# A list scheduler that models TensorE's tiles and keeps a sum of activity, and a state scaled on ScalarE

## The chip, the core and the metric

The kernel runs on one core of one Trainium2 chip. The metric is the device time of one execution in microseconds. Before the change three runs took 1821.65, 1817.13 and 1821.46 us, a median of 1821.46.

## What is computed

One layer of a hybrid trunk is applied to 512 tokens of a sample (with cached context) and to 128 tokens of a prompt, 640 rows of 1024 channels in all, in float32. In the reference, cut to what matters:

```
h   = rmsnorm(x) * (1 + scale1) + shift1                 # scale, shift, gate from silu(c) @ ada_w
u   = h @ w_in                                           # all branches' inputs and gates
y_a = latent attention(u)        y_b = mLSTM(u), both directions
y_c = windowed attention(u)      y_d = RWKV-7(u), both directions
x   = x + gate1 * ((sum of sigmoid(gate_i) * (y_i @ w_o_i)) @ w_out)
x   = x + gate2 * (relu(h2 @ mlp_w1)**2 @ mlp_w2)        # h2: the norm of the new x
```

The RWKV branch holds a 64 x 64 state S per head and direction, advanced token by token:

```
S_new = S * w_t - (S @ kh_t) (a_t kh_t)^T + v_t k_t^T,   y_t = S_new @ r_t
```

The last states and caches of the prompt are outputs too.

## The kernel before

Dense products are done three times with float32r operands: an operand is cut into a high part (`wh`, `yh`, `HH`) and the rest (`wl`, `yl`, `HL`), and high x high, high x low and low x high are summed (`mm3`). A weight tile comes by DMA into one of three buffers `wr`, ScalarE casts it to `wh` (line 589), and POOL for the first 139 tiles, VectorE for the others, forms `wl` (line 592); both have six buffers. `dense_b` (tiles `pb`, 320 columns), `dense_t` (`pt`, 208 to 264 columns) and `dense_a` (`pa`, 512 columns) then run the matmuls. Projections of `h` read `HH` and `HL`. Small products (RWKV, attention's probabilities, transposes) are plain float32 matmuls; the profile lists each of these as two instructions where it isn't a transpose.

The RWKV branch takes heads in pairs `hp`, each in two directions. `rwkv_prep` makes decayed keys, their products (`pat`, `pkb`, `pbs`) and masks; `rwkv_inverse` and `rwkv_comb` invert 32 x 32 blocks (`ptp`, `px`); `rwkv_chain` walks the chunks of 64 tokens. One `step` of it (from line 1100; 80 in all, 20 per pair, in four interleaved sequences) multiplies the old state `so_` (128 x 128, two heads) by `KR`, adds `Am` x `VU` on a 64 x 64 tile, copies the result to `W1` (ScalarE, line 1115), multiplies it on a 64 x 64 tile, negates it into `VU` (VectorE, line 1118), then runs four matmuls on 128 x 64 tiles, two for the output `ys` (ScalarE, line 1127) and two for the state. Line 1109 scales the old state by the decay `DL` into the new one `sn`, and line 1124 (VectorE) adds the product to it.

What sets the order of all this is a planner, `order`, at the end of the build. It reads every instruction, finds what each must wait for, gives it a duration (`cost`), and plays the program through: at each moment the engine that is free first takes, of its instructions whose inputs are there, the one with the longest path `bl` to the end. The resulting order per engine is written into the program; the chip runs each engine's queue in it. TensorE has one more rule: the planner adds up columns (`cols`) in the ticks of a fixed grid (`TICK`), holds TensorE to be slow in a tick when the one before had under 3060 (`warm`), and where the present tick seems to fall short it picks the matmul with the most columns per time. Conflicts of matmuls on the same rows and columns of the array are modelled in `busy`; a change of tile costs nothing, and the next matmul may be chosen 0.02 us after the last began. Projections that nothing needs soon (`late`, the gates above all) are put between the RWKV, mLSTM and attention work in this way.

Of the kernel before, what the change touches and what calls it, by code (L numbers as in the profile page):

```python
# [2 lines left out]

# [10 lines left out]
AF = mybir.ActivationFunctionType  # L14
ALU = mybir.AluOpType
# [19 lines left out]

LAT = {"PE": 0.3, "DVE": 0.195, "Activation": 0.195, "Pool": 0.195}
TO_PE = 0.127
DMA_START, DMA_END, DMA_RATE, DMA_GAP = 1.5, 0.95, 360e3, 0.641


# [86 lines left out]
def cost(i, eng, op, pools):  # L127

    ins = [q for q in i.ins if hasattr(q, "bass_ap")]
    outs = [q for q in i.outs if hasattr(q, "bass_ap")]  # L130

    def free(q):
        n = 1
        for s, c in list(q.ap)[1:]:
            n *= c
        return n

    def psum(q):
        t = pools.tiles.get(q.bass_ap.tensor.name)
        return t is not None and "PSUM" in t[0].space  # L140

    if op == "InstMatmult":
        n, m, k = free(outs[0]), list(outs[0].ap)[0][1], list(ins[0].ap)[0][1]
        if "is_transpose=True" in str(i):
            return 0.109
        if "float32r" in str(i.ins[0].dtype):
            return max(n / 2400, 0.107) + 0.003
        return max(n / 600, 0.05) + 0.002
        
    n = max([free(q) for q in ins + outs] or [1])  # L150
    if eng == "Activation":
        if op == "InstLoadActFuncSet":
            return 1.28
        return (0.051 if psum(ins[0]) else 0.094) + n / 1200 + 0.093 * (len(ins) + len(outs) - 2)
    if eng == "DVE":
        if op == "InstTensorScalarPtr":
            return 0.13 + n / 960 if 'is_scalar_tensor_tensor=True' in str(i) else 0.068 + n / (960 if psum(ins[0]) else 1920)
        if op == "InstTensorCopy" and not psum(ins[0]):
            return 0.068 + n / 1920
        return 0.066 + n / 960  # L160
    if eng == "Pool":
        if op == "InstDMACopy":
            return 1.04
        return 0.15 + n / (480 if op == "InstTensorTensor" else 240 if op == "InstTensorScalarPtr" else 800)
    return 0.05


def order(tc, pools):
    raw = list(tc.nc.cur_bb.bb.instructions)
    N = len(raw)  # L170
    eng = [str(i.engine).split(".")[-1] for i in raw]
    op = [type(i).__name__ for i in raw]
    live = [o != "BassTilePoolBoundary" for o in op]
    dur = [cost(i, e, o, pools) if l else 0.0 for i, e, o, l in zip(raw, eng, op, live)]
# [26 lines left out]
    for k, i in enumerate(raw):  # L201
# [11 lines left out]
        for q, wr in seq:  # L213
# [3 lines left out]
            t = pools.tiles.get(name)  # L217
# [10 lines left out]
            p0, p1, m = regions(q, dram)  # L228
            w, r = acc.setdefault(name, ([], []))
# [87 lines left out]
    while st:  # L317
        a = st.pop()
# [6 lines left out]
    for a in reversed(topo):  # L325
        x = 0.0
# [74 lines left out]
    for a in spot:  # L401
        q, i = raw[a].outs[0], raw[a].ins[0]
        n = 1
        for s, c in list(q.ap)[1:]:
            n *= c
        passes = 2 if "is_transpose=True" in str(raw[a]) else 1 if "float32r" in str(i.dtype) else 4
        cols[a] = passes * n * (spot[a][1] - spot[a][0]) / 128
    warm = lambda t: seen.get(int(t / TICK) - 1, 0) >= 3060
    while left:
        best = None  # L410
        for e in ENG:
            if avail[e]:
                t = free[e]
            elif future[e]:
                t = max(free[e], future[e][0][0])
            else:
                continue
            if best is None or t < best[0]:
                best = (t, e)
        t, e = best  # L420
        while future[e] and future[e][0][0] <= t + 1e-9:
            r, a = heapq.heappop(future[e])
            heapq.heappush(avail[e], (-bl[a], a))
        j = 0
        if e == "PE" and (0.937 or 0) and len(avail[e]) > 1:
            gap = 3060 - seen.get(int(t / TICK), 0)
            if (not warm(t) and 0) or gap > ((int(t / TICK) + 1) * TICK - t) * 2400 * 0.937 > 0:
                j = max(range(len(avail[e])), key=lambda i: (cols[avail[e][i][1]] / dur[avail[e][i][1]], -avail[e][i][0]))
        if j:
            _, a = avail[e].pop(j)  # L430
            heapq.heapify(avail[e])
        else:
            _, a = heapq.heappop(avail[e])
        start[a] = t
        if isdma[a]:
            by = 4
            for s, c in list(raw[a].outs[0].ap):
                by *= c
            if list(raw[a].outs[0].ap)[-1][1] < 128:
                by *= 2  # L440
            if e == "SP":
                hw = t + (DMA_GAP if raw[a].ins[0].bass_ap.tensor.name in pools.tiles and "DRAM" not in pools.tiles[raw[a].ins[0].bass_ap.tensor.name][0].space else 0.606)
            else:
                hw = t + 1.04
            b0 = max(bus, hw + DMA_START)
            bus = b0 + by / DMA_RATE
            fin = bus
            free[e] = hw
        else:
            if e == "PE":  # L450
                r0, r1, c0, c1 = spot[a]
                t = max([t] + [x[4] for x in busy if x[0] < r1 and r0 < x[1] and x[2] < c1 and c0 < x[3]])
                start[a] = t
                w = warm(t)
                fin = t + dur[a] * (1 if w else 2)
                k, x = int(t / TICK), t
                while x < fin:
                    y = min(fin, (k + 1) * TICK)
                    seen[k] = seen.get(k, 0) + cols[a] * (y - x) / (fin - t)
                    k, x = k + 1, y  # L460
                busy = [x for x in busy if x[4] > t + 0.02] + [(r0, r1, c0, c1, fin)]
                free[e] = t + 0.02
            else:
                fin = free[e] = t + dur[a]
        out[e].append(a)
        left -= 1
        for tl in of[a]:
            tdone[tl] = max(tdone.get(tl, 0.0), fin + (DMA_END if isdma[a] else 0.13))
            nuse[tl] -= 1
            if nuse[tl] == 0:  # L470
                P, key, _ = pools.tiles[tl]
                q = tags[id(P), key]
                heapq.heappush(q[0], (tdone[tl], tl))
                grant(q)
        for b, l in succ[a]:
            ready[b] = max(ready[b], (t if l < -1 else fin + l))
            need2[b] -= 1
            if need2[b] == 0:
                release(b)
    info = mybir.DependencyInfo(mybir.DependencyClass.NoSync, mybir.DependencyReason.DATA)  # L480
    for e in ENG:
        for a, b in zip(out[e], out[e][1:]):
# [41 lines left out]
def build(nc, tc, I, O):  # L524
# [562 lines left out]
    def rwkv_chain(units):  # L1087
# [13 lines left out]
        def step(ui, i):  # L1101
# [4 lines left out]
            sn = S[ui, sq] = stile()  # L1106
            VU = rp.tile([128, 128], F32, tag="VU", bufs=4, name=nm("VU"))
            SY.dma_start(VU[0:64, :], vscr[c * 64 : c * 64 + 64, ts_(hp)])
            G.tensor_scalar(sn, so_, DL[:, c : c + 1], None, op0=ALU.mult)  # L1109
            ps = mps.tile([128, 512], F32, tag="pc", bufs=PC, name=nm("pst"))  # L1110
            mm(ps[:, 0:128], KR[:, c, :], so_, start=True, stop=False)
            for h in range(2):
# [771 lines left out]
```

## Time and profile before

| | |
|---|---|
| median of three runs | 1821.46 us |
| profiled execution | 1829.33 us, span 1827.4 us |
| mean granted TensorE clock | 0.960 |
| TensorE busy | 1742.4 us, 95% |
| weight loads busy | 1551.1 us, 85% |
| VectorE busy | 968.7 us, 53% |
| ScalarE busy | 716.9 us, 39% |
| POOL busy | 471.9 us, 26% |

A busy time is the union of an engine's instructions; matmuls overlap, so a busy TensorE can still be a slow one, and starts a known distance apart tell more. The granted clock is a share of full speed. In groups of instructions `out<-in` are the program's tile names, then shapes and the count, busy time and the mean of one, and last the idle time of the engine before them with whom it waited for.

### The profile page before, as it was taken

What the parts mean: (1) busy time and instruction counts of PE and PEld (TensorE: products, weight loads), DVE (VectorE), ACT (ScalarE), POOL (GpSimd) and SP (SyncE); (2) the same over time, 40 slices, a digit from 0 to 9 for tenths busy, and PEclk for the clock granted to TensorE, in tenths of its full rate; (3) what the DMA queues carried; (4) which work ended last, traced back from release to release, by engine and by line L of the source; (5) the groups of instructions that cost most, each with busy time, mean ns of one, the idle gap of its engine ahead of it and who ended that gap; (6) DMA issues with size and microseconds to landing.
All of it is one profiled execution on the core that took longest, in us unless ns stands there. A gap on an engine that the chain in (4) does not pass through costs nothing.

```text
span 1827.4 us, 32001 instructions
## 1 busy us (share of the span) xinstructions
PE 1742.4 (95%) x11923; PEld 1551.1 (85%) x11923; DVE 968.7 (53%) x2250; ACT 716.9 (39%) x1711; POOL 471.9 (26%) x488
## 2 busy tenths in 40 slices
PE   6999899999999987999989999899999999999998
PEld 3998788888888876878887999799889899898997
DVE  4236937586363348665548654367744334343342
ACT  5543242333223224675635643354434223132231
POOL 3455543354233223331222211005100010202012
PEclk9999999898679998999999999999999999999999
DMA  8554352344224354533363211576512222222222
GB/s 291 153 180 122 103 132 74 90 118 108 64 59 122 114 170 149 168 89 65 86 159 105 74 41 56 167 253 221 173 45 81 68 77 70 81 76 75 76 74 94
DMA packets 243211, 206.66 MB, mean 113 GB/s; under 512 B 46086, under 2 KB 194360, under 8 KB 243056
## 3 DMA queue, kind: packets, MB, share of 16 engines
q1 hardware_dynamic: 242416, 204.07, 38.2%
q8 instruction: 94, 1.54, 0.4%
q0 software_dynamic: 640, 0.56, 0.1%
q14 instruction: 61, 0.50, 0.1%
HBM read 163.08 MB, written 41.49 MB: 112 GB/s over the span
## 4 chain that ended last, share of the span: by engine, by line
PE 57%; DVE 5%; DMA 5%; ACT 1%; issue 1%; SPq 0%; POOL 0%; POOLq 0%; DVEq 0%; ACTq 0%
PE pb L542 29%; PE pa L542 12%; PE pwo L542 2%; DMA out_new_mlstm_n<-co 2%; PE pst L542 2%; PE pas L542 2%; PE pat L542 2%; PE pat L565 1%; PE pso L542 1%; PE pmo L542 1%; PE psc L542 1%; PE pada L542 1%; DMA wr<-in_w_in 1%; PE pms L542 1%; PE pspt L565 0%
## 5 line engine op out<-in xcount | busy, mean ns | idle before, releaser
L542 PE MATMUL pb<-HH,wh 128*128 128x320 f32 x1328 | 364.1, 325 | 21.8 <-ACT spb L833 10.8
L542 PE MATMUL pb<-HL,wh 128*128 128x320 f32 x1328 | 359.5, 323 | 0.8 <-DVE HL L753 0.8
L542 PE MATMUL pb<-HH,wl 128*128 128x320 f32 x1328 | 356.0, 321 | 0.0
L589 ACT CAST wh<-wr 128x512 fp32r<-128x512 f32 (+2 forms) x298 | 183.5, 618 | 379.9 <-PE pa L542 144.2
L592 POOL TENSOR_TENSOR wl<-wr,wh 128x512 fp32r<-128x512 f32 (+2 forms) x139 | 187.4, 1352 | 415.0 <-ACT wh L589 307.8
L542 PEld LDWEIGHTS pb<-HH,wh 128*128 128x128 f32 x1328 | 237.5, 192 | 33.6 <-ACT spb L833 12.9
L542 PEld LDWEIGHTS pb<-HL,wh 128*128 128x128 f32 x1328 | 236.8, 192 | 7.3 <-issue 4.0
L542 PEld LDWEIGHTS pb<-HH,wl 128*128 128x128 f32 x1328 | 236.4, 192 | 6.3 <-issue 3.5
L592 DVE TENSOR_TENSOR wl<-wr,wh 128x512 fp32r<-128x512 f32 x159 | 117.4, 744 | 200.1 <-ACT wh L589 116.5
L1846 POOL TENSOR_TENSOR x<-x,yt 128x512 f32<-128x512 f32 x40 | 53.6, 1341 | 480.7 <-DVE yt L1845 473.7
L542 PE MATMUL pt<-wh,HH 128*128 128x256 f32 (+2 forms) x360 | 101.7, 318 | 7.8 <-DVE mift L860 5.4
L542 PE MATMUL pa<-wh,fh 128*128 128x512 f32 x320 | 108.1, 393 | 0.0
L542 PE MATMUL pa<-wh,fl 128*128 128x512 f32 x320 | 106.7, 393 | 0.0
L542 PE MATMUL pa<-wl,fh 128*128 128x512 f32 x320 | 104.9, 393 | 0.0
L542 PE MATMUL pt<-wh,HL 128*128 128x256 f32 (+2 forms) x360 | 97.9, 312 | 0.0
L542 PE MATMUL pt<-wl,HH 128*128 128x256 f32 (+2 forms) x360 | 96.8, 310 | 0.0
L1109 POOL TENSOR_SCALAR S<-S,DL 128x128 f32<-128x128 f32 x80 | 56.8, 714 | 126.9 <-DVE S L1124 100.3
L542 PEld LDWEIGHTS pt<-wh,HH 128*128 128x128 f32 x360 | 68.1, 206 | 13.6 <-DVE mift L860 3.0
L835 DVE COPY spb<-pb 128x320 f32<-128x320 f32 x46 | 22.4, 487 | 105.9 <-PE pb L542 105.7
L542 PE MATMUL pst<-VU,Am 128*64 128x64 f32 (+1 forms) x640 | 74.2, 242 | 0.9 <-DVE VU L1118 0.5
L542 PE MATMUL pb<-yh,wh 128*128 128x320 f32 x256 | 64.8, 318 | 10.0 <-ACT yh L1752 6.5
L542 PEld LDWEIGHTS pa<-wh,fh 128*128 128x128 f32 x320 | 60.1, 188 | 13.4
(535 smaller groups left out, 3587.0 us busy)
## 6 DMA issues: line engine op xcount, KB each, us to landing
wr<-in_mlp_w SPq DMA_DIRECT2D x128, 256.0 KB
wr<-in_w_in SPq DMA_DIRECT2D x122, 256.0 KB
wa<-in_ada_w SPq DMA_DIRECT2D x64, 256.0 KB
gtd<-spb SPq DMA_DIRECT2D x32, 320.0 KB
sg<-gtd SPq DMA_DIRECT2D x32, 320.0 KB
ara<-in_ada_w SPq DMA_DIRECT2D x16, 512.0 KB
sgd<-sg SPq DMA_DIRECT2D x16, 320.0 KB
la<-sgd SPq DMA_DIRECT2D x16, 320.0 KB
```

The costliest lines, as they stand in the source:

```text
L542: PE.matmul(out, lhsT, rhs, start=start, stop=stop)
L565: PE.transpose(out, in_, ident[: in_.shape[0], : in_.shape[0]])
L589: A.copy(hi[:, :n], raw[:, :n])
L592: e.tensor_tensor(lo[:, :n], raw[:, :n], hi[:, :n].bitcast(F32), op=ALU.subtract)
L835: V.tensor_copy(t[:, hs(h)], p)
L1109: G.tensor_scalar(sn, so_, DL[:, c : c + 1], None, op0=ALU.mult)
L1846: G.tensor_tensor(x2[tt][:, cs], x2[tt][:, cs], t, op=ALU.add)
```

## The change

In `cost`, durations are changed: TensorE's float32r matmul from columns / 2400 + 0.003 (at least 0.110) to columns / 2300 + 0.008 (at least 0.111), its float32 matmul also by the rows of the output, and some of VectorE's, ScalarE's and POOL's. In `order`, TensorE's columns are weighted by the output columns that a matmul fills; a change of the tile's form costs 0.14 us and waits until all running matmuls are done, a plain float32 matmul after one that isn't costs 0.08; the engine is taken until the weights are loaded. The sum of activity is taken over a rolling tick that ends now (`past`), at every choice. Under 4000, the matmul with the most columns per time, the cost of a change included, is taken; above it, the most urgent, where one of another form counts as 40 us less urgent (`STAY`). In `step`, ScalarE scales the state in POOL's place. The diff's core:

```diff
+STAY = 40.0
+FLOOR, FULL = 4000, 4000
 def cost
         if "float32r" in str(i.ins[0].dtype):
-            return max(n / 2400, 0.107) + 0.003
-        return max(n / 600, 0.05) + 0.002
+            return max(n / 2300 + 0.008, 0.111)
+        return max(n, (n + m) / 2) / 600 + 0.005
...
+            if "Scan" in str(i) or "scan=True" in str(i):
+                return 0.066 + n / 480
...
+        if op == "InstTensorTensor" and not any(psum(q) for q in ins):
+            return max(0.066 + n / 960, 0.09) * 1.12
+        return max(0.066 + n / 960, 0.09)
...
-        return 0.15 + n / (480 if op == "InstTensorTensor" else 240 if op == "InstTensorScalarPtr" else 800)
+        if op == "InstMemset":
+            return 0.02 + n / 1150
+        return 0.15 + n / (450 if op == "InstTensorTensor" else 220 if op == "InstTensorScalarPtr" else 800)
 def order
-        cols[a] = passes * n * (spot[a][1] - spot[a][0]) / 128
-    warm = lambda t: seen.get(int(t / TICK) - 1, 0) >= 3060
+        cols[a] = passes * n * (spot[a][1] - spot[a][0]) / 128 * (0.5 + (spot[a][3] - spot[a][2]) / 256)
+    warm = lambda t: seen.get(int(t / TICK) - 1, 0) >= 3040
+    fit = lambda n: 32 if n <= 32 else 64 if n <= 64 else 128
+    form, load = {}, {}
+    for a, (r0, r1, c0, c1) in spot.items():
+        slow = "is_transpose=True" not in str(raw[a]) and "float32r" not in str(raw[a].ins[0].dtype)
+        form[a] = (fit(r1 - r0), fit(c1 - c0)), slow
+        load[a] = (c1 - c0) / 1200 * (2 if slow else 1)
+    now, trail = ((128, 128), False), deque()
+    turn = lambda a: 0.14 if form[a][0] != now[0] else 0.08 if form[a][1] and not now[1] else 0.0
...
-            gap = 3060 - seen.get(int(t / TICK), 0)
-            if (not warm(t) and 0) or gap > ((int(t / TICK) + 1) * TICK - t) * 2400 * 0.937 > 0:
-                j = max(range(len(avail[e])), key=lambda i: (cols[avail[e][i][1]] / dur[avail[e][i][1]], -avail[e][i][0]))
+            while trail and trail[0][1] <= t - TICK:
+                trail.popleft()
+            past = sum(c * (y - max(x, t - TICK)) / (y - x) for x, y, c in trail)
+            if past < (FLOOR if warm(t) else FULL):
+                j = max(range(len(avail[e])), key=lambda i: (cols[avail[e][i][1]] / (dur[avail[e][i][1]] + turn(avail[e][i][1])), -avail[e][i][0]))
+            else:
+                j = min(range(len(avail[e])), key=lambda i: avail[e][i][0] + (STAY if form[avail[e][i][1]][0] != now[0] else 0.0))
...
-                t = max([t] + [x[4] for x in busy if x[0] < r1 and r0 < x[1] and x[2] < c1 and c0 < x[3]])
+                other = form[a][0] != now[0]
+                t = max([t] + [x[4] for x in busy if other or x[0] < r1 and r0 < x[1] and x[2] < c1 and c0 < x[3]]) + turn(a)
+                now = form[a]
+                trail.append((t, t + dur[a] * (1 if warm(t) else 2), cols[a]))
...
-                free[e] = t + 0.02
+                free[e] = t + max(0.02, min(fin - t, load[a] * (1 if w else 2)))
 def step
-            G.tensor_scalar(sn, so_, DL[:, c : c + 1], None, op0=ALU.mult)
+            A.activation(sn, so_, AF.Copy, scale=DL[:, c : c + 1])
```

## Rows read from the trace of the kernel before

**Rows 1.** The page: busy time per engine; granted clock in tenths over forty slices.
```profile
PE 1742.4 (95%) x11923; PEld 1551.1 (85%) x11923; DVE 968.7 (53%) x2250; ACT 716.9 (39%) x1711; POOL 471.9 (26%) x488
...
PEclk9999999898679998999999999999999999999999
```

**Rows 2.** Stretches by stage (length, busy per engine with count, clock, DMA share, GB/s).
```profile
180.00:340.00 160.00, 151.27 (x1326) 132.39 (x1324) 112.47 (x240) 53.84 (x111) 69.44 (x63) 0.99 0.39 105
...
670.00:740.00 70.00, 57.09 (x334) 49.44 (x334) 50.95 (x119) 26.00 (x62) 23.92 (x30) 0.80 0.51 157
...
950.00:1180.00 230.00, 228.28 (x1648) 215.90 (x1650) 136.81 (x392) 110.57 (x299) 36.13 (x32) 1.00 0.29 85
...
1320.00:1827.40 507.40, 499.63 (x2746) 447.44 (x2744) 199.22 (x350) 146.66 (x310) 53.58 (x40) 1.00 0.25 77
```

**Rows 3.** The twelve stretches at a low clock, and their sum.
```profile
343.00:357.00 14.00, 14.00 (x95) 12.27 (x93) 4.46 (x9) 4.48 (x10) 1.27 (x1) 0.51 0.22 50
442.00:493.00 51.00, 51.00 (x368) 45.54 (x368) 15.87 (x36) 8.11 (x22) 9.06 (x11) 0.50 0.30 74
511.00:534.00 23.00, 23.00 (x122) 19.64 (x121) 11.69 (x30) 2.41 (x9) 5.66 (x6) 0.50 0.18 48
...
708.00:722.00 14.00, 8.11 (x28) 6.66 (x29) 13.63 (x31) 2.37 (x9) 2.01 (x3) 0.51 0.47 142
...
1186.00:1193.00 7.00, 4.11 (x14) 3.71 (x15) 5.67 (x8) 4.33 (x8) 0.00 (x0) 0.52 0.91 306
sum 146.00, PE 134.37 PEld 118.56 DVE 76.39 ACT 36.65 POOL 30.34; mean PE 11.20 PEld 9.88 DVE 6.37 ACT 3.05 POOL 2.53
```

**Rows 4.** TensorE's waits: for whom, us in total, times, longest.
```profile
PE pnt L565 <- DVE rst L576: 12.3, 1, 12.3
PE pb L542 <- ACT spb L833: 10.8, 4, 5.5
```

**Rows 5.** The stages again, instructions that read or write HH alone.
```profile
180.00:340.00 160.00, 85.08 (x394) 61.89 (x393) 0.00 (x0) 0.00 (x0) 0.00 (x0) 0.99 0.39 105
...
442.00:494.00 52.00, 16.57 (x50) 12.77 (x50) 0.00 (x0) 0.00 (x0) 0.00 (x0) 0.51 0.30 74
...
534.00:670.00 136.00, 66.05 (x284) 46.26 (x283) 0.00 (x0) 0.00 (x0) 0.00 (x0) 1.00 0.45 126
...
950.00:1180.00 230.00, 116.84 (x460) 77.10 (x460) 0.00 (x0) 0.00 (x0) 0.00 (x0) 1.00 0.29 85
```

**Rows 6.** TensorE's groups from 442 to 493 us (count, busy us, mean ns, idle).
```profile
L542 PE MATMUL pt<-wh,HH 128*128 128x208 f32 x24 | 9.2, 451 | 0.0
...
L542 PE MATMUL pat<-KR,KB 64*128 64x128 f32 x40 | 7.8, 446 | 0.0
L542 PE MATMUL px<-Am,TP 32*32 32x32 f32 x80 | 5.1, 237 | 0.0
```

**Rows 7.** TensorE in order of time around 610 us (start, length).
```profile
609.71 0.31 PE L542 MATMUL pb<-HH,wl 128*128 128x320 f32 x1
609.86 0.30 PE L542 MATMUL pb<-HL,wh 128*128 128x320 f32 x1
610.10 0.82 PE L542 MATMUL pst<-VU,Am 128*64 128x64 f32 x8
```

**Rows 8.** Groups of instructions: the POOL scaling, two ScalarE operations of that size.
```profile
L1109 POOL TENSOR_SCALAR S<-S,DL 128x128 f32<-128x128 f32 x80 | 56.8, 714 | 126.9 <-DVE S L1124 100.3 <-DMA rk<-rkd 9.6 <-PE pst L542 5.3
...
L1340 ACT ACTIVATE hd<-pmo,dn 128x128 f32<-128x128 f32 x20 | 7.3, 364 | 4.9 <-DVE dn L1338 2.4 <-PE pyb L565 2.3
...
L1344 ACT ACTIVATE jk<-hd 128x128 f32<-128x128 f32 x20 | 6.2, 308 | 1.5 <-DVE hd L1341 1.4
```

**Rows 9.** Waits of all engines from 60 to 680 us.
```profile
ACT W L1115 <- PE pst L542: 77.0, 61, 4.5
...
ACT ys L1127 <- DVE S L1124: 57.2, 34, 4.3
...
PEld pst L542 <- issue: 13.9, 72, 0.8
```

More of the change, by code (lines that the diff above doesn't have):

```diff
@@ L1 @@
 import heapq
+from collections import deque
 from contextlib import ExitStack, contextmanager
@@ L153, in cost @@
             return 1.28
-        return (0.051 if psum(ins[0]) else 0.094) + n / 1200 + 0.093 * (len(ins) + len(outs) - 2)
+        return (0.051 if psum(ins[0]) and n > 128 else 0.094) + n / 1200 + 0.093 * (len(ins) + len(outs) - 2)
     if eng == "DVE":
         if op == "InstTensorScalarPtr":
-            return 0.13 + n / 960 if 'is_scalar_tensor_tensor=True' in str(i) else 0.068 + n / (960 if psum(ins[0]) else 1920)
+            if "Scan" in str(i) or "scan=True" in str(i):
+                return 0.066 + n / 480
+            return 0.14 + n / 960 if 'is_scalar_tensor_tensor=True' in str(i) else 0.068 + n / (960 if psum(ins[0]) else 1920)
         if op == "InstTensorCopy" and not psum(ins[0]):
             return 0.068 + n / 1920
-        return 0.066 + n / 960
+        if op == "InstTensorTensor" and not any(psum(q) for q in ins):
+            return max(0.066 + n / 960, 0.09) * 1.12
+        return max(0.066 + n / 960, 0.09)
     if eng == "Pool":
@@ L479, in order @@
                 release(b)
+    order.span = max(free.values())
     info = mybir.DependencyInfo(mybir.DependencyClass.NoSync, mybir.DependencyReason.DATA)
```

## The prediction

> **What bounds the kernel now.** I read the busy table first, then the stages, then the clock, then TensorE's waits. TensorE is busy for 95% of the span, its weight loads for 85%, and no other engine passes 53% [rows 1]. Cut into thirteen stages from 60 us on, of which four stand here, it is over 90% busy in all but one (670 to 740 us, 82%); the last 507 us, from the output projection on, are 98% busy at full clock [rows 2]. So TensorE sets the end, and time can come back in three ways only: less time at the low clock, fewer pauses between unlike matmuls, fewer waits. Every other edit counts only through these.
>
> The line of clock tenths dips most in slices 10 to 12 [rows 1]; cut finely, there are twelve stretches at about 0.50, 146 us in all (0.50 is the level of 1.2 GHz, 1.00 that of 2.4 GHz) [rows 3]. They are of two kinds. In three of them, in the middle of the RWKV stage (14, 51 and 23 us), TensorE is busy the whole time: it doesn't lack work, it has the wrong mix. In the others (58 us) something around them is late: at 708 us TensorE is busy for 8.1 of 14 us, at 1186 us for 4.1 of 7. The waits proper are small: 1827.4 - 1742.4 = 85 us of idle, the largest 12.3 us at the start, then a tail of a few us each [rows 4].
>
> **a. The activity sum (the new floor and the rolling window): the main term.** What tells the warm RWKV stretches from the cold ones is how much dense projection work runs between the small matmuls. Of matmuls that read HH (two thirds of the projections) there are 394 in the 160 us from 180 on and 284 in the 136 us from 534 on, 2.5 and 2.1 per us; in the cold 52 us from 442 on there are 50, 1.0 per us [rows 5]. In their place that stretch holds two groups of 80 32x32 matmuls (one of them stands here), 40 of 64 rows, and projections only 208 columns wide [rows 6]. The old planner picked by density only near the end of each tick of a fixed grid, with every matmul dated too short (below). The new one looks back over a rolling tick at every choice, discounts matmuls that fill few output columns, and asks for 4000 where the old rule asked for 3060. It would put projections between those small matmuls. There are enough: from 950 to 1180 us, long after RWKV, 460 that read HH are still to run [rows 5], and moved forward each costs the same where the clock is full.
>
> Price: the time lost in the three stretches is length times (1 - clock): 14 x 0.49 + 51 x 0.50 + 23 x 0.50 = 43.9 us [rows 3]. I take three quarters, 33 us, since the order is fixed beforehand and will run off its plan somewhere. Bounds: 44 us if all three go; below nothing if other stretches turn cold (rival C). In the other nine and at the start some 29 us is lost (1827.4 x (1 - 0.960), the mean clock, is 73 in all); they begin where data is late, which no pick on TensorE mends: 3 us, bounds 0 and 10.
>
> In the cold stretch at 442 us TensorE is busy for 51.00 of 51.00 us and still granted 0.50 [rows 3]. The Trainium skill ("TensorE: Matmul & The Clock Gate", section "HAM oscillation — how this bites in real kernels") puts the fall down to gaps in which TensorE idles behind a transfer. By that rule alone a choice between matmuls that are all ready would leave the clock where it is, and this term would be zero; the trace here speaks against it, though it fits the stretches at 708 and 1186 us. It is rival A.
>
> **b. Durations on TensorE.** Projection matmuls of 320 columns start 0.14 to 0.15 us apart [rows 7]; the old formula gives 320/2400 + 0.003 = 0.136, the new 320/2300 + 0.008 = 0.147. So the old plan ran some 7% ahead of the chip in all dense work and placed its other engines' work against a wrong clock. What a truer plan is worth is in the waits: of 85 us idle, the largest single one is at the start and stays. I take 3 us, bounds -10 (a reordered queue makes new waits) and +15 (about a fifth of the idle).
>
> **c. Tile changes (STAY and the turn cost).** A 320-column matmul starts 0.145 us after its like; a 128x64 small one that follows it starts 0.24 us after it, so entering a small tile costs 0.095 us [rows 7]. In the sequencer's list the same shows as 72 small stalls before RWKV matmuls, 13.9 us, a lower bound [rows 9]. A step of the chain enters small tiles three times (the 64x64 pair on VU, the 64x64 pair on W1, the 128x64 four), so 80 steps make at most 240 entries and as many exits: 240 x 0.095 = 23 us, and up to as much again for the exits. The new rule holds on to a shape unless another matmul is 40 us more urgent. That joins like steps of the four interleaved sequences, but a chain matmul is usually far more urgent than a projection, so most changes stay. I take a quarter of 23 to 46 us: 8 us, bounds 0 and 23 (half of 46). Price on the other side: a chain matmul can be held back by others of the present shape. The chain is not what ends last while projections remain, so the cover is those projections, and it ends where they run out.
>
> **d. The state's scaling moves from POOL to ScalarE.** It removes 80 POOL instructions, 56.8 us [rows 8]. On ScalarE 128x128 from SBUF costs 308 ns (a square with a sum) and 364 ns with a per-row scale from PSUM [rows 8]: 80 x 0.31 to 0.36 = 25 to 29 us, on an engine that is 39% busy [rows 1]. It is not on the path: only the last update of the state needs it, after three rounds of TensorE, ScalarE and VectorE; and ScalarE's queue already waits for this chain (77.0 us for W1, 57.2 us for the state before ys) [rows 9]. Behind the waiting scale stand the weight casts to wh, and behind these POOL's differences and the projections; three raw weight buffers and six split ones cover a wait of a few us. POOL in return no longer holds its differences behind 100.3 us of waiting for the state [rows 8]. Value 0, bounds -5 (a cast held up at a few of 80 steps, 1 us each) and +5.
>
> The other new costs (POOL, VectorE scans, small ScalarE operations) change orders on engines that are half idle: 0, within the bounds of b. The DMA queue of SP is planned with the same constants; its order shifts only as the work before it does, and the head's loads are chained as they were.
>
> **Sum.** 33 + 3 + 3 + 8 + 0 = 47 us off the profiled execution's 1829.3 us (its span of 1827.4 and 1.9 around it): 1782.3. That execution lies 7.9 us above the median of the runs, 1821.5, so on their scale it is 1774.4 us. With all upper bounds, 44 + 10 + 15 + 23 + 5 = 97, it would be 1725; I don't expect them together.
>
> **Rivals.**
> A. The clock follows TensorE's idle time, not its mix. For: the cold spots at 708 and 1186 us begin in idle. Against: 88 us of cold with TensorE fully busy [rows 3]. Only b and c remain: 1821.5 - 11 = 1810 us. The section of the Trainium skill named under a would lead here. Chance 0.06.
> B. The cold stretches move. The chip leaves the plan through late weights or transfers, and what is cured at 442 us returns elsewhere: a third of the 44 us is kept and c's 8 us partly lost to holding back. 1821.5 - 10 = 1811 us, spread 1800 to 1824. For: the old plan also counted on enough activity in each tick and missed it for 88 us. Chance 0.14.
> C. Slower: a fall of the clock locks in. While it is at 1.2 GHz the same order brings half as many columns per us, so an order that spreads the projections evenly, just above the floor, holds no dense burst that lifts it again; the stretch at 442 us lasted 51 us in this way. The place is RWKV from 180 to 670 us, 490 us long, of which 88 are cold now. Each further cold us costs 0.5 us, and b and c give 11 us back, so it decides from 88 + 22 = 110 us of cold; with 170 us it is 41 - 11 = 30 us slower, 1851 us. For: one such fall exists; against: the floor is a third above the old one. Chance 0.12.
> D. More than forecast, most upper bounds at once, below 1745 us. Chance 0.06.
>
> **How the numbers follow.** The forecast, 1774.4 us, has 0.62; its own range is 1745 to 1800. Below 1742 and above 1824 lie about 0.18 together, so the range is 1742 to 1824. A difference under 0.3%, 5.5 us, is no change that a measurement of this kernel can tell. Faster by more: 0.62 + 0.06 (D) + 0.05 of A + 0.09 of B = 0.82. Within 0.3%: 0.01 of A and 0.05 of B = 0.06. Slower: C, 0.12.
>
> **What would show it.** Right: no stretch at 0.50 longer than about 10 us between 180 and 670 us; total cold time down from 146 to some 70 to 80 us; HH matmuls at about 2 per us throughout RWKV and fewer than 460 in the 230 us before the output stage; fewer entries into small tiles; ScalarE some 27 us busier, POOL 57 us less; the last 507 us [rows 2] unchanged. Wrong in a: the cold total stays near 146 us or the stretches have moved. Wrong in c: as many changes of tile as before. Wrong in d: casts to wh that wait on the state's update, and TensorE waiting for them. Wrong altogether: TensorE idle for well over 85 us, because a chain held back starves what follows RWKV.

## The result and the profile after

The changed kernel takes 1943.8 us, the median of four runs (1927.4 to 1958.0), against 1821.6 us for four of the kernel before. Here and below, a run more than 1.5% above the fastest of its kernel is left out of every comparison; here that is the one at 1958.0, and the median of the other three is 1935.7 us: 1.063 times as long, interval 1.052 to 1.074. Forecast were 1774.4 us and a gain. The profiled execution is the one of 1935.7 us, its span 1933.9; that of before lay 8 us over its median, so between the two spans are 106.5 us, between the medians 114.

The page of the kernel after, busy time by engine and the granted clock in forty slices:

```profile
PE 1816.8 (94%) x11923; PEld 1599.0 (83%) x11923; DVE 974.1 (50%) x2250; ACT 745.0 (39%) x1791; POOL 415.6 (21%) x408
...
PEclk9999959967958699999889999998999999999999
```

Beside [rows 1]: the same matmuls take 74.4 us more of TensorE, ScalarE has 28.1 us more and POOL 56.3 us less, as the move of the scaling should give. The clock line now has four dips in slices 6 to 14 where it had one. The span was cut at the end of the recurrence, the last matmul into `pst`: 649.4 us before, 700.2 us after. First before, then after (length, busy per engine, clock, DMA share, GB/s):

```profile
60.00:180.00 120.00, 115.21 (x833) 109.81 (x832) 49.01 (x71) 52.56 (x96) 58.84 (x56) 1.00 0.53 162
180.00:649.40 469.40, 455.43 (x3879) 389.21 (x3878) 273.63 (x640) 147.61 (x350) 179.02 (x185) 0.90 0.37 99
649.40:1320.00 670.60, 626.41 (x4232) 574.20 (x4230) 418.86 (x1117) 339.63 (x895) 155.48 (x177) 0.96 0.45 130
```

```profile
60.00:180.00 120.00, 110.73 (x793) 104.13 (x792) 56.15 (x78) 52.27 (x98) 57.21 (x53) 1.00 0.51 153
180.00:700.20 520.20, 494.81 (x3691) 405.29 (x3691) 264.51 (x626) 166.16 (x416) 115.15 (x101) 0.78 0.31 80
700.20:1427.00 726.80, 671.12 (x4492) 615.74 (x4491) 428.58 (x1133) 349.26 (x911) 163.80 (x184) 0.96 0.46 133
1427.00:1933.90 506.90, 494.93 (x2708) 442.12 (x2707) 198.03 (x341) 146.38 (x306) 54.95 (x40) 0.99 0.23 70
```

The recurrence takes 50.8 us longer, though TensorE runs 188 matmuls fewer in it; 260 more are left for the stage behind it, which takes 56.2 us longer at the same mean clock. The last 507 us are as before [rows 2]. So two things happened: the recurrence ran slow, and it did less of the other work meanwhile.

How slow shows in the stretches at the low level, 0.50 or 1.2 GHz, of the kernel after in that stage. The six of at least 10 us stand here; two more are 3.4 us each:

```profile
240.80:295.40 54.60, 53.72 (x266) 41.70 (x267) 5.56 (x18) 8.52 (x20) 9.01 (x9) 0.50 0.24 67
380.80:411.50 30.70, 30.52 (x171) 23.61 (x172) 6.43 (x16) 6.18 (x15) 3.90 (x3) 0.50 0.18 47
425.00:452.30 27.30, 27.30 (x147) 21.41 (x146) 19.87 (x49) 7.12 (x21) 1.54 (x1) 0.50 0.28 81
459.00:469.20 10.20, 9.66 (x55) 7.88 (x55) 9.82 (x20) 2.79 (x8) 4.45 (x3) 0.51 0.20 53
537.80:592.40 54.60, 53.96 (x324) 44.05 (x325) 34.17 (x103) 17.49 (x49) 0.20 (x1) 0.50 0.17 44
623.00:660.50 37.50, 37.50 (x217) 31.64 (x217) 8.01 (x22) 7.00 (x20) 5.30 (x4) 0.50 0.19 55
sum 214.90, PE 212.65 PEld 170.28 DVE 83.86 ACT 49.10 POOL 24.40; mean PE 35.44 PEld 28.38 DVE 13.98 ACT 8.18 POOL 4.07
```

214.9 us, where the three stretches before were 88 us [rows 3]; and again TensorE is busy for 212.65 us of them. What it does there, in the last one (groups of TensorE: count, busy us, mean ns, idle):

```profile
L567 PE MATMUL pt<-wl,HH 128*128 128x208 f32 x26 | 10.8, 448 | 0.0
...
L567 PE MATMUL px<-Am,TP 32*32 32x32 f32 x40 | 4.2, 242 | 0.0
L567 PE MATMUL ptp<-XT,Am 32*32 32x32 f32 x30 | 3.0, 241 | 0.0
```

That is the stretch at 442 us over again [rows 6]: narrow projections and blocks of 32. The projections that read `HH`, after, by stage (instructions that read or write HH alone), and last the whole recurrence, first before, then after:

```profile
180.00:340.00 160.00, 82.18 (x300) 0.81 0.31 85
...
540.00:670.00 130.00, 61.41 (x224) 0.65 0.30 78
950.00:1180.00 230.00, 112.80 (x469) 0.94 0.36 94
...
180.00:649.40 469.40, 217.53 (x928) 0.90 0.37 99
180.00:700.20 520.20, 225.63 (x816) 0.78 0.31 80
```

300 where there were 394 in the first 160 us; between 950 and 1180 us 469 where there were 460 [rows 5]. Over the whole recurrence from 180 us on there were 928 and are 816. I had forecast the opposite on every one of these counts.

TensorE's waits, after (us in total, times, longest):

```profile
PE pyb L590 <- ACT co L1387: 12.5, 3, 5.3
PE pnt L590 <- DVE x L765: 12.4, 1, 12.4
PE pb L567 <- DVE spb L860: 9.2, 8, 3.4
...
PE pb L567 <- ACT wh L614: 6.9, 1, 6.9
```

The wait at the start is the old one [rows 4]; behind it the waits are smaller and more. All idle together is 1933.9 - 1816.8 = 117.1 us, 32.1 more than before.

**An account.** Each span can be split into three: lost to the clock, span x (1 - mean clock); idle, span - TensorE's busy time; and the rest, work at full clock with its changes of tile. Before: 73.1 + 85.0 + 1669.3. After: 150.8 + 117.1 + 1666.0. So of the 106.5 us the clock has 77.7, idle time 32.1, the rest -3.3. (The split charges the clock for all of a slow stretch, also for what there doesn't follow the clock; where much is lost, the rest comes out somewhat low. The clock is given to three places, so each term is good to about 1 us.)

One execution's split is a draw. Over 38 executions of the kernel before in the rounds of the experiments, all with the same order, span x (1 - mean clock) goes from 46.9 to 78.7 us, 63.2 on the mean, while idle and rest together stay between 1748.2 and 1759.3, mean 1753.9. So the trace of before stands at the upper end for the clock. Three executions of the kernel after have 151.8 (136.7 to 167.7) and 1784.8. On these means the clock has 89 us of a difference of 119, idle and rest 31; and a difference of some ten us in one trace's lost time shows nothing by itself.

### The profile page after: what moved, and what is told of

Its sections match the earlier page's. It is cut to its first block, busy times and chain, and to the rows that moved or that the text cites. A ratio compares the mean times of both kernels' runs of the same rounds, so it can differ in the third digit from the quotient of the medians.

```text
span 1933.9 us, 31904 instructions
## 1 busy us (share of the span) xinstructions
PE 1816.8 (94%) x11923; PEld 1599.0 (83%) x11923; DVE 974.1 (50%) x2250; ACT 745.0 (39%) x1791; POOL 415.6 (21%) x408
## 4 chain that ended last, share of the span: by engine, by line
PE 59%; DMA 5%; DVE 5%; ACT 3%; issue 1%; POOL 0%; SPq 0%; POOLq 0%; ACTq 0%; DVEq 0%
PE pb L567 27%; PE pa L567 11%; PE pt L567 4%; PE pst L567 3%; PE pwo L567 3%; DMA out_new_mlstm_n<-co 2%; PE pat L567 2%; PE pas L567 2%; PE pat L590 1%; DMA rk<-yscr 1%; PE psc L567 1%; DMA Mb<-mdr 1%; PE pso L567 1%; PE pmo L567 1%; PE pms L567 1%
## 5 line engine op out<-in xcount | busy, mean ns | idle before, releaser
L567 PE MATMUL pb<-HH,wh 128*128 128x320 f32 x1328 | 374.2, 326 | 18.3 <-DVE spb L860 9.2
L567 PE MATMUL pb<-HH,wl 128*128 128x320 f32 x1328 | 364.7, 321 | 0.3 <-DVE wl L617 0.3
L567 PE MATMUL pt<-wh,HH 128*128 128x256 f32 (+2 forms) x360 | 113.3, 354 | 10.3 <-DVE spb L860 3.7
L567 PE MATMUL pa<-wl,fh 128*128 128x512 f32 x320 | 114.4, 394 | 0.0
L567 PE MATMUL pt<-wh,HL 128*128 128x256 f32 (+2 forms) x360 | 110.3, 347 | 0.0
L567 PE MATMUL pt<-wl,HH 128*128 128x256 f32 (+2 forms) x360 | 108.0, 346 | 0.0
L567 PE MATMUL pst<-VU,Am 128*64 128x64 f32 (+1 forms) x640 | 84.9, 265 | 0.8 <-DVE VU L1143 0.8
L567 PEld LDWEIGHTS pst<-VU,Am 128*64 128x64 f32 (+1 forms) x640 | 60.6, 163 | 22.0 <-issue 11.2
L567 PEld LDWEIGHTS pt<-wh,HL 128*128 128x128 f32 x360 | 75.1, 228 | 4.3
L567 PEld LDWEIGHTS pt<-wl,HH 128*128 128x128 f32 x360 | 74.2, 229 | 4.8
```

Of the source, the lines that this page charges most:

```text
L567: PE.matmul(out, lhsT, rhs, start=start, stop=stop)
```

## The experiments

Three theories. **The price** (M in the expectations): the plan that charges TensorE for changes of tile and for weight loads believes that it has little time to spare, so it puts fewer projections between the chain's matmuls, and in such a thin order a fall of the clock lasts longer. **The scaling** (S): ScalarE's copy holds up the chain and the casts, and the waits bring the clock down. **The rule of choice** (H, F): the rolling sum, its level or `STAY` pick badly. And behind all three **luck** (L): any new order is some per cent better or worse by where its waits fall.

The account of every run (lost, idle and rest of the profiled execution, us; HH: matmuls that read it from 180 us to the end of the recurrence). The ratio is taken against the runs of before in the same rounds, whose medians lie between 1814 and 1822 us. The execution profiled for e5 took 1847.3 us, 15 us more than its median, so its lost time is high for it:

| run | median us | ratio to before, 95% | lost | idle | rest | HH |
|---|---|---|---|---|---|---|
| before | 1821.6 | | 73.1 | 85.0 | 1669.3 | 928 |
| after | 1935.7 | 1.052 to 1.074 | 150.8 | 117.1 | 1666.0 | 816 |
| e1_tiles_unpriced | 1812.8 | 0.992 to 0.999 | 61.3 | 79.3 | 1663.8 | 898 |
| e2_pool_scale | 1903.3 | 1.034 to 1.060 | 123.5 | 116.7 | 1660.2 | 766 |
| e3_stay0 | 1975.9 | 1.074 to 1.100 | 177.8 | 103.1 | 1695.0 | 887 |
| e4_floor5000 | 1998.0 | 1.085 to 1.114 | 101.6 | 133.9 | 1756.5 | 1330 |
| e5_turn_zero | 1831.8 | 1.001 to 1.012 | 97.8 | 88.7 | 1658.8 | 813 |
| e6_turn_half | 1892.8 | 1.023 to 1.054 | 118.7 | 96.4 | 1669.2 | 705 |
| e7_before_lat | 1829.3 | 1.000 to 1.010 | 63.7 | 93.5 | 1662.9 | 929 |
| e8_before_act | 1844.9 | 0.996 to 1.028 | 94.4 | 94.0 | 1662.8 | 910 |
| e9_unpriced_pool | 1796.9 | 0.979 to 0.994 | 75.9 | 80.4 | 1651.2 | 904 |
| e10_old_pick | 1973.1 | 1.073 to 1.090 | 236.7 | 105.2 | 1630.8 | 372 |
| e11_unpriced_pool_5000 | 1872.2 | 1.015 to 1.031 | 118.0 | 103.6 | 1651.4 | 923 |
| e12_unpriced_pool_oldcost | 1790.0 | 0.974 to 0.986 | 57.3 | 83.5 | 1649.3 | 907 |
| e13_before_turn | 1878.1 | 1.018 to 1.044 | 146.8 | 87.2 | 1647.7 | 555 |
| e14_after_lat | 1887.9 | 1.023 to 1.049 | 113.0 | 112.7 | 1657.0 | 711 |
| e15_best_lat | 1802.3 | 0.986 to 0.996 | 59.4 | 85.6 | 1655.7 | 912 |
| e16_5000_lat | 1853.4 | 1.005 to 1.030 | 94.3 | 91.1 | 1664.1 | 933 |

### Taking the price away

e1: the kernel after, with no price for a change of tile, no wait for running matmuls at one, and the next matmul 0.02 us after the last again.

```diff
-    turn = lambda a: 0.14 if form[a][0] != now[0] else 0.08 if form[a][1] and not now[1] else 0.0
+    turn = lambda a: 0.0
...
-                t = max([t] + [x[4] for x in busy if other or x[0] < r1 and r0 < x[1] and x[2] < c1 and c0 < x[3]]) + turn(a)
+                t = max([t] + [x[4] for x in busy if x[0] < r1 and r0 < x[1] and x[2] < c1 and c0 < x[3]]) + turn(a)
...
-                free[e] = t + max(0.02, min(fin - t, load[a] * (1 if w else 2)))
+                free[e] = t + 0.02
```

> The changed kernel with the tile model taken out of the planner: a change of tile costs nothing, doesn't wait for the running matmuls, and TensorE may be given its next matmul 0.02 us after the last began, as before the change; durations, floor 4000, STAY 40 and the ScalarE scaling stay. Theory M (thin mix): with small matmuls priced in full the RWKV chain fills TensorE's time, fewer projections go between, the floor holds the mix only just where the clock holds, and once it falls the order can't lift it again. Unpriced, the plan has free time on TensorE again and puts more projections in: cold time from 180 to 670 us falls from about 220 us to under 100, HH matmuls from 180 to 670 rise from 768 towards the 993 of before, time 1790 to 1850 us. Rivals: H (STAY holds chain matmuls back) and S (the scaling blocks ScalarE's queue) both expect 1920 to 1960 us, since these stay in. Rival L (any new order of this program is that bad, the old one was a lucky draw): 1900 to 1960 us.

1812.8 us: the whole loss of 114 us is gone with these three lines. The recurrence is short again, and its clock is 0.92 for 0.78:

```profile
180.00:618.40 438.40, 423.93 (x3815) 367.74 (x3814) 263.33 (x628) 167.80 (x420) 117.11 (x103) 0.92 0.38 100
```

Against the kernel before, the clock is not better: on the mean of all executions e1 loses 69.9 us to it, before 64.3 in the same rounds. e5 and e6 give the dose, with `turn` alone changed (wait and load charge kept). First e5, then e6:

```diff
-    turn = lambda a: 0.14 if form[a][0] != now[0] else 0.08 if form[a][1] and not now[1] else 0.0
+    turn = lambda a: 0.0
...
+    turn = lambda a: 0.07 if form[a][0] != now[0] else 0.04 if form[a][1] and not now[1] else 0.0
```

> The changed kernel with one part of the tile model taken out: a change of tile, and a plain float32 matmul after a float32r one, cost the planner nothing (0 instead of 0.14 and 0.08); it still waits for the running matmuls and still holds TensorE until the weights are in. M, sharpened: it is the price of the turn that takes the plan's free time on TensorE away, so this alone brings most of the first run back: 1805 to 1850 us, cold time from 180 to 670 us under 120 us. If instead the occupancy by weight loads does it: 1900 us or more. L (luck of the order): anything from 1800 to 1980 us, unrelated to the projections placed.

> The changed kernel with the turn at half price, 0.07 and 0.04. M: a dose between, 1820 to 1915 us, with projections before the chain's end and cold time between those of the changed kernel and of the run without the price. L: no order among the three.

1831.8 us at no price, 1892.8 at half, 1935.7 at the full one. Between none and half the step is clear; between half and full it isn't, since the full price in another order (e14, under Luck) takes 1887.9. What the wait and the load charge still cost would be 1831.8 - 1812.8 = 19 us, no more than another order can make. HH doesn't follow the dose here (813, 705, 816), so the count alone isn't the measure of the mix. The times lie where the theory of the price (M) had them; e5's 144 us at the low level in its recurrence (under 120 expected) and e6's HH, below both its neighbours, do not.

e13 is the reverse: the kernel before, with nothing but the price added.

```diff
+    turn = lambda a: 0.14 if form[a][0] != now[0] else 0.08 if form[a][1] and not now[1] else 0.0
...
-                t = max([t] + [x[4] for x in busy if x[0] < r1 and r0 < x[1] and x[2] < c1 and c0 < x[3]])
+                t = max([t] + [x[4] for x in busy if x[0] < r1 and r0 < x[1] and x[2] < c1 and c0 < x[3]]) + turn(a)
+                now = form[a]
```

> The kernel before, its planner's TensorE charged 0.14 us for a change of tile and 0.08 for a plain float32 matmul after a float32r one; old durations, old choice, state on POOL. M: the price alone thins the mix, and with the weak old rule of choice nothing puts projections back: 1890 us or more, cold time from 180 to 670 us over 180 us. If the loss needs the new rule of choice (floor, STAY): 1800 to 1850 us.

1878.1 us, 3.1% slower than before (1.8 to 4.4%): M had 1890 or more, the rival at most 1850. Its recurrence, in the columns of the stages:

```profile
180.00:639.60 459.60, 432.13 (x3298) 358.76 (x3297) 264.99 (x623) 128.86 (x313) 151.18 (x163) 0.74 0.28 75
```

581 matmuls fewer than before in that stage, 555 on HH, and a clock of 0.74 for 0.90. All idle time is 87.2 us, as before (85.0): here the loss is of the clock alone, and it comes with the price by itself. But within the recurrence idle time has doubled, 459.60 - 432.13 = 27.5 us for 469.40 - 455.43 = 14.0, so a thinner mix and more waits come together.

### The scaling

e2 is the kernel after with the state scaled on POOL, e8 the kernel before with it on ScalarE.

```diff
-            A.activation(sn, so_, AF.Copy, scale=DL[:, c : c + 1])
+            G.tensor_scalar(sn, so_, DL[:, c : c + 1], None, op0=ALU.mult)
```

> The changed kernel with the state scaled on POOL again, all of the new planner kept. M: the mix stays thin, 1915 to 1965 us, cold time within 50 us of 277. S: the casts no longer wait behind the state, 1850 us or less. H and L: 1915 to 1965 us.

> The kernel before with the state scaled on ScalarE and the old planner. M and my account of that part: 1800 to 1840 us, ScalarE some 25 to 32 us busier. S (the scaling blocks ScalarE's queue): 1860 us or more, with casts to wh that wait for the state's update.

With POOL in place of ScalarE 1903.3 against 1935.7 us, in the kernel before 1821.6 against 1844.9 (ratio 1.012, 0.996 to 1.028); e9 below gives 1796.9 against e1's 1812.8. Three times POOL is better by 1 to 2%, though e8's interval includes no change, and each pair is two orders as well. The forecasts for these pairs were not met: e2 lies 12 us below M's range, e8 5 us above it and 15 below that of S, and e9's 1796.9 falls between its two answers, so the third pair decided nothing. It is a small part: on POOL the changed kernel still loses 82 us. Nor do the waits speak for a mechanism. After, the operation and its own wait (groups of instructions, then waits):

```profile
L1134 ACT ACTIVATE S<-S,DL 128x128 f32<-128x128 f32 x80 | 30.3, 399 | 8.3 <-DVE S L1149 8.0
```

ScalarE waits 8.0 us for the state, and TensorE 6.9 us for a cast, once.

### The rule of choice

e10 puts the old rule back into the kernel after, prices kept (`STAY` goes with the new rule); e3 takes `STAY` to 0; e4 raises the level.

```diff
-            past = sum(c * (y - max(x, t - TICK)) / (y - x) for x, y, c in trail)
-            if past < (FLOOR if warm(t) else FULL):
...
+            gap = 3060 - seen.get(int(t / TICK), 0)
+            if (not warm(t) and 0) or gap > ((int(t / TICK) + 1) * TICK - t) * 2400 * 0.937 > 0:
+                j = max(range(len(avail[e])), key=lambda i: (cols[avail[e][i][1]] / dur[avail[e][i][1]], -avail[e][i][0]))
```

```diff
-STAY = 40.0
+STAY = 0.0
```

```diff
-FLOOR, FULL = 4000, 4000
+FLOOR, FULL = 5000, 5000
```

> The changed kernel with the old rule of choice on TensorE (fixed ticks, looked at near their end, no STAY), prices of tiles and all else kept. M: the prices thin the mix and nothing but that weak rule puts projections back, so RWKV runs cold nearly throughout: cold time from 180 to 670 us 300 us or more, 1960 us or more, slower than the changed kernel. If the new rule of choice (floor and STAY) is itself what thins the mix: 1850 us or less.

> The changed kernel with STAY 0 instead of 40. M: no projection more is put in, 1900 to 1970 us, cold time over 200 us; entries into small tiles rise a little. H: the chain is freed and ends well before 700 us, 1850 us or less. S, L: 1900 to 1970 us.

> The changed kernel with both floors at 5000 instead of 4000. M: between 180 and 500 us the projections come thicker and cold time there falls from about 150 us to under 50; but the chain is pushed later and the projections run out sooner, so some cold and idle time comes back between 550 and 800 us; 1830 to 1900 us. H, S, L: 1915 us or more, cold time as before.

All three are slower than the kernel after, e10 and e3 by 2%, which another order can make too, e4 by 3%. M had e10 right; e3 lies 6 us above its range, and e4, forecast at 1830 to 1900 us, is a plain miss. e10 shows what the price makes of a plan that doesn't watch activity closely: 372 matmuls on HH and, in the 130 us from 540 us on, the low level throughout with TensorE busy (e10, stages):

```profile
540.00:670.00 130.00, 128.84 (x756) 97.13 (x755) 40.88 (x126) 37.66 (x109) 10.35 (x12) 0.50 0.22 57
```

So the new rule does what term a said: with the prices in place it brings 816 where the old one brings 372, and 237 us lost to the clock fall to 151. Of these 86 us the span keeps 39, as rest (35 us) and idle (12 us) grow. The price takes more than the rule gives. In e3 the matmuls' forms change 934 times, against 760 after and 667 before (a form is a matmul's rows and columns of the array, each rounded up to 32, 64 or 128; counted in the trace's matmul records), and rest and clock are both worse. e4 does cure the clock in the recurrence (its stages):

```profile
180.00:868.00 688.00, 657.04 (x4578) 503.01 (x4578) 269.85 (x649) 194.43 (x467) 157.08 (x134) 0.93 0.35 98
868.00:1180.00 312.00, 251.10 (x1545) 215.97 (x1542) 209.97 (x710) 172.56 (x561) 74.30 (x111) 0.89 0.30 85
```

at 0.93; but the chain now ends at 869 us, what follows has TensorE busy for 251 of 312 us, forms change 1146 times and the rest is 90.5 us above that of the kernel after. In this pair a high level on a priced plan buys the clock with the chain. e11 asks whether the level hurts without the price.

### Without the price

e9 is e1 with the state on POOL, both edits as above. e11 is e9 with the level of e4. e12 is e9 with the whole of `cost` as before, so that of the change only the weighted columns, the rolling sum, 4000 and `STAY` are left; its core:

```diff
-            return max(n / 2300 + 0.008, 0.111)
-        return max(n, (n + m) / 2) / 600 + 0.005
+            return max(n / 2400, 0.107) + 0.003
+        return max(n / 600, 0.05) + 0.002
```

> The run without the tile model (1812.8 us) with the state scaled on POOL again: new durations, floor, STAY and rolling sum stay. Third pair for the scaling, after 1943.8 against 1903.3 and 1844.9 against 1815.2 us: if ScalarE's 30 us of scaling costs 1 to 2% wherever it stands, 1778 to 1795 us; if those two pairs were only other orders, 1800 to 1830 us. M expects at most 1830 us in both cases.

> Without the tile model, state on POOL, both floors 5000. M: the floor is rarely reached in a plan with a thick mix, so it does little and costs few changes of tile: within 1.5% of the run with 4000. Rival F (a higher floor always starves the chain, as it did with the prices, 1998 us): 1870 us or more.

> Without the tile model, state on POOL, and the durations of before: of the change only the weighting of columns, the rolling floor and STAY are left. If the truer durations are worth something beside the floor, this is slower than the run with them by 5 us or more; M by itself expects the mix to be as thick or thicker, 1780 to 1825 us. If the rolling floor is what cures the cold stretches, cold time from 180 to 670 us is under 80 us here too.

e12 is faster than both kernels: 1790.0 us, 0.980 of before (0.974 to 0.986). Its recurrence, and its six stretches at the low level there, the first and the longest of them:

```profile
180.00:620.60 440.60, 424.35 (x3828) 368.57 (x3827) 277.43 (x635) 144.04 (x345) 175.73 (x181) 0.92 0.38 102
...
211.60:225.30 13.70, 13.70 (x60) 12.31 (x60) 8.46 (x16) 3.03 (x6) 1.30 (x1) 0.50 0.38 105
...
450.50:477.80 27.30, 27.30 (x216) 24.14 (x215) 9.69 (x24) 6.39 (x19) 4.99 (x8) 0.50 0.34 93
...
sum 68.30, PE 68.19 PEld 59.90 DVE 31.13 ACT 13.70 POOL 14.69; mean PE 11.37 PEld 9.98 DVE 5.19 ACT 2.28 POOL 2.45
```

The clock falls about as often as in the kernel after (six times against eight), but a fall lasts 68.3 / 6 = 11 us on the mean, there 221.7 / 8 = 28 us. Against the kernel before it is the other way about: three falls of 88 / 3 = 29 us there [rows 3], so what grew with the change is their number, not their length. Of the 37.3 us by which e12's profiled span is shorter than that of before, the clock has 15.8, idle 1.5 and the rest 20.0; forms change 569 times for 667. On the means of the executions the clock has only 8 us (54.8 for 63.2, inside the range of before) and idle and rest 21 (1732.6 for 1753.9): most of e12's gain is not the clock's. e9 and e12 differ in the durations alone, and their intervals overlap.

e11 is the run that the theory of the price missed: without a price 5000 was to cost next to nothing, and it costs 1872.2 - 1796.9 = 75 us against e9. Its HH count (923) and rest (1651.4) are good, its clock isn't (118.0 us lost). Why more activity asked for brings less isn't settled.

### Luck

To see what a new order alone does, one constant of the planner, VectorE's latency, was moved by 5 ns in four kernels: before (e7), after (e14), e12 (e15) and e11 (e16).

```diff
-LAT = {"PE": 0.3, "DVE": 0.195, "Activation": 0.195, "Pool": 0.195}
+LAT = {"PE": 0.3, "DVE": 0.200, "Activation": 0.195, "Pool": 0.195}
```

> The kernel before with one harmless number of its planner moved: the latency after a VectorE instruction 0.200 instead of 0.195 us. It makes another order out of the same rules and is the control for luck. M: within 2% of before, 1785 to 1855 us, since the mix stays thick. L: the old order was a lucky draw, so 1870 us or more.

> The changed kernel with the latency after a VectorE instruction 0.200 instead of 0.195 us in its planner. M: another order from the same rules, still thin: 1880 to 1980 us. L (a draw): may be anywhere, below 1850 us as likely as not.

> The fastest version so far (no tile prices, state on POOL, durations of before; weighting, rolling floor and STAY of the change kept, 1790.0 us) with the same move of the latency. If its gain is the rolling floor's: 1775 to 1812 us, faster than before again. If a draw: 1815 us or more.

> No tile prices, state on POOL, floors 5000 (1872.2 us) with the same move of the latency. If that loss was scatter (falls of the clock that happened to lock in): 1785 to 1840 us here. If the higher floor does it (it lets projections run out or holds the chain up): 1850 to 1895 us again.

Before goes by +0.5%, after by -2.5% (1935.7 to 1887.9 us), e12 by +0.7%, e11 by -1.0%. No verdict turns: the changed kernel is still 2.3 to 4.9% slower than before, e12 still faster (0.4 to 1.4%), 5000 still slower. But two fifths of the loss of 114 us, and more than a third of e12's gain of 2%, lies within what another order can give or take, and a difference under some 3% between two priced plans, e2's and e3's among them, shows no cause by itself. What does is the sorting of all: eight plans with a price for turns (after, e2, e3, e4, e6, e10, e13, e14) take 1878.1 to 1998.0 us, eight without one and with a level of at most 4000 (before, e1, e5, e7, e8, e9, e12, e15) 1790.0 to 1844.9; the two do not touch, and the two at 5000 without a price (e11, e16) lie between them. The projections sort in the same way once the length of the stage and its clock are taken out: per us of the recurrence at full clock (HH over length x mean clock) the eight with a price run 1.29 to 2.09, the ten without one 2.13 to 2.25. So the price thins the order; that much is shown.

What the runs don't show is by which step the price thins the order (that the plan then sees less free time on TensorE is my reading of the code), whether the thinner mix or the added waits in the recurrence (14.0 us of idle before, 25.4 after) bring the clock down, and what exactly in an order lifts it again. Nor is it settled how much of the harm comes of a price set too high: 0.14 us stands for every change, where [rows 7] give 0.095 us for an entry; but at 0.07 (e6) the kernel is 3.8% slower than before, too.

## Why the prediction was wrong

**The view of the bound** held. TensorE sets the end, and the account closes with clock, idle and rest; the last 507 us didn't move.

**Term a (33 us off; it became 78 us on, 89 on the means)** is the step that failed, in the sentence "It would put projections between those small matmuls". I priced the rolling sum as if it stood alone. In the same diff a change of tile costs 0.14 us, and among the chain's small matmuls a projection is such a change; a priced plan puts fewer there. e10 and the kernel after show the sum at work (372 to 816), e13 the price at work (928 to 555), e12 and e15 the sum without the price: 54.8 and 56.8 us lost to the clock on the mean of their executions, for 63.2 before. That is 6 to 8 us of the 33, and inside the range of before; so the size was wrong as well, and that the sum cures the clock at all is not shown. I also read the old plan's free changes of tile as an error that mending would improve. They went with projections dense among the chain's matmuls. That its short durations did the same isn't shown.

**Term b (3 us)** can't be told from nothing: e9 and e12, 1796.9 and 1790.0 us, overlap.

**Term c (8 us, bounds 0 and 23)** was sized by the changes that would go, and as such is roughly there where no price stands beside it: e12's rest is 20.0 us smaller, e15's 13.6, e1's 5.5. That `STAY` does it isn't shown: no run takes it out of an unpriced plan. In the kernel after nothing went: the rest is 3.3 us smaller, forms change 760 times for 667, and the list of waits from 60 to 680 us has

```profile
PEld pst L567 <- issue: 19.8, 91, 0.5
```

where it had 13.9 us in 72 [rows 9]. The cover that I named, projections that remain while a chain matmul is held back, was there; what I left out is that the same price pushes the projections out.

**Term d (0; 25 to 29 us of ScalarE)**: 80 operations took 30.3 us, 399 ns each, above both bounds [rows 8]. The waits that I feared are small (8.0 and 6.9 us), the three pairs lean to 1 or 2% against ScalarE, which is more than my bound of 5 us; beside the scatter above it stays open.

**Rival C** is nearest to what happened, with 0.12 and 1851 us. Its place (180 to 670 us) and its sign were right, and stretches do stay low with TensorE busy. But its reason, an order spread evenly just above the floor, was not the price; and a fall that locks in was there before, 29 us on the mean, while the change brought more of them. Its size was not right either: I took 170 us of cold time in that stage, and there are 214.9 + 2 x 3.4 = 221.7, so (221.7 - 88) / 2 = 67 us for 41; b and c were to give 11 us back and gave 3; and idle, 32 us, was not in it. Idle over 85 us was my sign for "wrong altogether", though the chain held back was to starve what follows; 11.5 us of the 32 lie behind the recurrence, 11.4 in it.

**Rival A**, idle only, is half right, and the half is worth knowing. The 4 us ahead of each of the six stretches (kernel after, the first three):

```profile
236.80:240.80 4.00, 3.35 (x33) 2.52 (x32) 3.97 (x4) 1.40 (x3) 3.55 (x2) 0.99 0.26 66
376.80:380.80 4.00, 2.00 (x16) 1.42 (x15) 1.55 (x3) 0.66 (x2) 0.00 (x0) 0.98 0.43 122
421.00:425.00 4.00, 2.34 (x18) 1.70 (x17) 3.82 (x7) 1.24 (x5) 1.99 (x2) 1.00 0.08 19
```

In all six TensorE is busy for 2.0 to 3.35 of 4 us, as in only one in seven of the stretches of 4 us at full clock in that stage: at 376.8 it stands 2.2 us behind one matmul that waits for VectorE's `Am`, with projections queued behind it in the fixed order. So here waits stand ahead of the falls. That the mix then decides how long one lasts is a reading: e4, with 1.93 HH per us, has 13 falls of 8 us on the mean in its recurrence, e10, with 0.75, 6 of 69 us, at much the same idle time there (31 and 28 us); but before has 1.98 and falls of 29 us. The Trainium skill ("TensorE: Matmul & The Clock Gate", section "HAM oscillation — how this bites in real kernels") has the clock throttled by waits for a transfer between groups of matmuls; the six starts agree with it in so far as idle time stands ahead of them, the 212.65 busy us of 214.9 at the low level don't follow from it. Nor is idle time always there:

```profile
339.00:343.00 4.00, 4.00 (x36) 3.04 (x34) 1.78 (x4) 0.27 (x1) 1.76 (x3) 1.00 0.64 140
...
351.00:355.00 4.00, 4.00 (x50) 3.23 (x49) 1.37 (x3) 1.86 (x6) 1.54 (x2) 1.00 0.12 29
...
555.80:559.80 4.00, 4.00 (x62) 3.21 (x60) 1.97 (x6) 1.93 (x6) 0.00 (x0) 1.00 0.10 25
```

The first is the kernel before, ahead of the stretch at 343 us (ahead of the one at 442 us TensorE was busy for 2.49 of 4 us); the others are e1, ahead of falls at 355.0 and 559.8 us. Of e1's eight falls in the recurrence four begin so.

## What to carry to other kernels

A planner's errors can hold each other up: before a cost model is made truer, ask what its errors were good for, and price the truer cost and the new rule in the same diff against each other, not one after the other. Where the clock falls with TensorE busy, read a slow stretch twice, once for what TensorE waited for just before it and once for what it runs inside it, and take the clock's loss from many executions: here one order lost 47 to 79 us. And before an order is called better, move a harmless constant: here 5 ns in one latency moved a kernel by 2.5%.

## What the runs showed of the hardware

- The granted clock stayed at 0.50 for up to 54.6 us (537.8 to 592.4 us) with TensorE busy for 53.96 of them, and in e10 for all of 130 us with TensorE busy for 128.84.
- A wait isn't needed for a fall: before the stretch at 343 us, in the kernel before, TensorE was busy for all of the 4 us ahead of it, and so it was ahead of four of e1's eight falls.
- The same order loses a different time to the clock in each execution: 46.9 to 78.7 us in 38 executions of the kernel before, while the rest of its time stays within 11.1 us.
- ScalarE's scaled copy of 128x128 from SBUF takes 399 ns, where the same shape from PSUM took 364 and a square with a sum from SBUF 308 [rows 8].
